# A hybrid attention layer on one Trainium2 core: later slices for one gate weight's preparation, earlier ones for four other weights, and a later first banded score

## The chip, the cores and the metric

The kernel runs on one core of one Trainium2 chip, as one launch. The metric is device time in microseconds (us), the median of several runs; lower is better. One further execution was recorded by the hardware profiler, and all views quoted here are of that execution. Engines carry the profile's names: PE is the matrix engine, PEld its weight load, DVE the vector engine, ACT the scalar engine, POOL the GpSimd engine, SP the engine that only issues transfers. A name with a q behind it (SPq, POOLq) is that engine's issuing side.

## The reference

One decoder layer: an adaLN-modulated RMS norm, one combined input projection, two attention branches with SiLU gates, one output projection, a post-norm and a gated residual. Sizes: 2048 rows, width 1024, head width 64, 8 heads in each branch, 2 key/value heads in the banded one.

```python
mod = jax.nn.silu(c) @ w_ada[l] + b_ada[l]
shift, scale, gate = jnp.split(mod, 3, axis=-1)
h = rms_norm(x, g_pre[l]) * (1.0 + scale[:, None, :]) + shift[:, None, :]
proj = h @ w_in[l]
qa, ka, va, fa, za, qb, kb, vb, zb = jnp.split(proj, split_points, axis=-1)
oa = forgetting_attention(qa, ka, va, fa + b_fgate[l]) * jax.nn.silu(za)   # causal, gate bias
ob = sliding_window_sink_attention(rope(qb), rope(kb), vb, sinks[l]) * jax.nn.silu(zb)  # band of 128
y = jnp.concatenate([oa, ob], axis=-1) @ w_out[l]
x = x + gate[:, None, :] * rms_norm(y, g_post[l])
```

(The head reshapes are left out.)

## The kernel before

**Number format.** Every matmul operand is split into two half-precision parts, high and low, and three products (high by high, high by low, low by high) are added in one accumulation. A weight block of 1024 by 128 (a "key" such as `zb1`, the second tile of the banded branch's gate weight) must therefore be measured and split before its first matmul. Eight steps do this. `w_load` fetches the raw block (POOL's queue, L205). `w_max` takes the largest magnitude of each partition on DVE (L211) and POOL writes these 128 numbers to DRAM (`mx_d`, L214). `w_back` has POOL read them back, spread over all partitions (`mxr`, L219). `w_scale` reduces them to one number on DVE (L230) and makes a power-of-two scale from it (L86 to L237). `w_high` makes the high part on ACT (L245). `w_low`, in two halves, makes the low part on DVE (L251). `w_done` derives a factor from the scale.

**First stage.** The start section computes the modulation, a bound `bmx` on its result (L615, reduced over partitions through two small PE operations), and from it the scale and shift columns `Gp`, `Shp` that ACT applies to the transposed activations (L396). DVE splits the result into `hT` (L400, L401). Then the projections follow in a list `punits` of *slices*. A slice is a handful of matmuls: one eighth of a projection of 512 rows, or one transposition of a later group of 512 rows (`turn_x`). The list begins with 512-row group 0: eight slices of `kb` (slices 0 to 7), eight of `vb` (8 to 15), eight of `zb0` and eight of `zb1`, with eight transposition slices for group 1 set between them, so that `zb1` begins at slice 29 and group 1's `kb` at slice 40.

**What sets the order.** Inside `manual_schedule` the instructions of each engine are issued in the order in which the program writes them, up to small shifts between neighbouring steps. `add` puts the eight steps of a key into `events` at fixed numbers of slices ahead of the key's first slice (the leads). `fill(n, each)` runs n slices, the events of each slice first. `after(k, f)` defers a step by k ticks, and `tick2` ticks at every second slice. Every engine works through its own list strictly in order, so an instruction that waits holds up all that stand behind it on its engine.

**First banded scores.** After the first stage, 32 `windows` (pairs of 128-query blocks) are worked through: `scores` on PE (L831, into `pss`), `maxima` on DVE (L844), `exps` on ACT (L855), `turn` (PE transposes, L864, into `pxb`), `pv` (L883). Between them stand the remaining projection slices. Window 0's scores need the rotated queries `stb`, which come from ACT (high part, L713) and DVE (low part, L706) after a transfer that swaps half-heads (`qs<-qf`, L699) and a POOL product (L711).

Of the kernel before, what the change touches and what calls it, by code (L numbers as in the profile page):

```python
# [40 lines left out]
def hybrid_layer(  # L41
# [158 lines left out]
    def w_load(key, pieces, eng=None):  # L200
        width = VB if key == "vb" else P
        raw = (vbw if key == "vb" else wpool).tile([P, KT, width], F32, tag="wraw", name=f"wr_{key}")
        o = 0
        for col0, n in pieces:
            (eng or G).dma_start(raw[:, :, o:o + n], w_in0[:, col0:col0 + n].rearrange("(k p) n -> p k n", p=P))  # L205
            o += n
        wq[key] = [raw]

    def w_max(key):
        mx = sm(1, "w_mx")  # L210
        V.tensor_reduce(mx[:], wq[key][0][:], axis=AX.XY, op=ALU.max, apply_absolute_value=True)  # L211
        md = mx_d[len(kaps_seen) % 3]
        kaps_seen.append(key)
        G.dma_start(md[:], mx[:])  # L214
        wq[key].append(md)

    def w_back(key):
        mxr = mxp.tile([P, P], F32, tag="mxr", name="mxr")
        G.dma_start(mxr[:], wq[key].pop().rearrange("p o -> (p o)").partition_broadcast(P))  # L219
        wq[key].append(mxr)  # L220

    def w_scale(key):

        floor = key[:2] == "qk"
        raw, mxr = wq[key]
        if key in first:
            mx2 = mxr
        else:
            mx2 = sm(1, "w_mx2")
            V.tensor_reduce(mx2[:], mxr[:], axis=AX.X, op=ALU.max)  # L230
        pw = sm(1, "w_pw")
        pow2_floor(pw[:], mx2[:], "w_p2")
        if floor:
            V.tensor_tensor(pw[:], pw[:], pfl[:], op=ALU.max)
        sw = sm(1, "w_sw")
        V.reciprocal(sw[:], pw[:])
        V.tensor_scalar(sw[:], sw[:], 2.0 ** 14, None, op0=ALU.mult)  # L237
        wq[key] = [raw, pw, sw]

    def w_high(key):  # L240
        raw, pw, sw = wq[key]
        width = VB if key == "vb" else P
        pool = vbw if key == "vb" else wpq if key[0] in "qk" else wpool
        whl = pool.tile([P, 2, KT, width], F16, tag="whl", name=f"wh_{key}")
        A.activation(whl[:, 0], raw[:], AF.Identity, scale=sw[:])  # L245
        wq[key].append(whl)

    def w_low(key, part, parts=2):
        raw, pw, sw, whl = wq[key]
        ks = slice(KT * part // parts, KT * (part + 1) // parts)  # L250
        V.scalar_tensor_tensor(whl[:, 1, ks], raw[:, ks], sw[:], whl[:, 0, ks], op0=ALU.mult, op1=ALU.subtract)  # L251
        if part == parts - 1:
            wq[key] = whl
            pws[key] = pw
# [34 lines left out]
    def pieces(key):  # L289
        kind, j = key[:2], int(key[2:] or 0)  # L290
        if kind == "vb":
            return [(OFF_VB, P), (OFF_FA, 8)]
        if kind == "qk":
            return [(OFF_QA + j * 64, 64), (OFF_KA + j * 64, 64)]
        return [({"qb": OFF_QB, "kb": OFF_KB, "va": OFF_VA, "za": OFF_ZA, "zb": OFF_ZB}[kind] + j * P, P)]
# [604 lines left out]
    def add(key, us):  # L900
        if key not in pkeys and key not in ("kb", "vb"):
            at = len(punits) - (24 if key[:2] == "za" else 0)
            for n, (lead, f) in enumerate(((42, lambda: w_load(key, pieces(key))), (31, lambda: w_max(key)),
                                           (21, lambda: w_back(key)), (12, lambda: w_scale(key)),
                                           (8, lambda: w_high(key)), (6, lambda: w_low(key, 0)),
                                           (4, lambda: w_low(key, 1)), (3, lambda: w_done(key)))):
                if key == "zb0":
                    if n >= 3:
                        events.setdefault(n + 9, []).append(f)
                else:  # L910
                    events.setdefault(max(at - lead, n), []).append(f)
        if key not in pkeys:
            pkeys.append(key)
        punits.extend(us)

    events = {}
    others = []
    for kind, j in (("zb", 0), ("zb", 1), ("va", 0), ("zb", 2), ("zb", 3), ("va", 1), ("va", 2)):
        key = f"{kind}{j}"
# [48 lines left out]
    N_PRO = len(punits)  # L968
# [72 lines left out]

    swa_order = tc.manual_schedule()
    with swa_order:
        fill(N_PRO - 4, tick2)
        psx.close()
        sws = swa_pool("sws", 1)
        ptp = swa_pool("ptp", 1)
        ps_s = swa_pool("ps_s", 1, space=PSUM)
        ps_t = swa_pool("ps_t", 1, space=PSUM)
        ps_pv = swa_pool("ps_pv", 1, space=PSUM)  # L1050
        wsp = swa_pool("wsp", 2)
        wss, wst = sm(16, "a_m"), sm(2, "wst")
        wsq = {}
        base = N_PRO
        NW = len(windows)
        windows[0].scores()
        windows[0].maxima()
        fill(2, tick2)
        windows[0].exps()
        fill(2, tick2)  # L1060
        for n, wd in enumerate(windows):
            goal = base + (N_SWA - base) * (n + 1) // NW
            todo = goal - pos[0]
            part = [todo * (m + 1) // 4 - todo * m // 4 for m in range(4)]
            tick()
            if n:
                wd.maxima()
            fill(part[0])
            tick()
            if n:  # L1070
                wd.exps()
            fill(part[1])
            tick()
            fill(part[2])
            tick()
            fill(part[3])
            if n:
                windows[n - 1].pv()
            wd.turn()
            if n + 1 < NW:  # L1080
                windows[n + 1].scores()

            if n:
                A.activation(wsq[n - 1][:], wsq[n - 1][:], AF.Square, accum_out=wss[:, (n - 1) % 16:(n - 1) % 16 + 1])
            if n == 16:
                V.tensor_reduce(wst[:, 0:1], wss[:], axis=AX.X, op=ALU.add)
            wsq[n] = wsp.tile([P, 2 * P], F32, tag="wsq", name="wsq")
            SP.dma_start(wsq[n][:], w_out0[n // 4 * P:(n // 4 + 1) * P, n % 4 * 2 * P:(n % 4 + 1) * 2 * P])
        tick()
        fill(5)  # L1090
        tick()
        fill(5)
        tick()
        fill(6)
        windows[NW - 1].pv()
        tick()
        tick()
        A.activation(wsq[NW - 1][:], wsq[NW - 1][:], AF.Square, accum_out=wss[:, 15:16])
        V.tensor_reduce(wst[:, 1:2], wss[:], axis=AX.X, op=ALU.add)
        wsum = sm(1, "w_mx2")  # L1100
        V.tensor_reduce(wsum[:], wst[:], axis=AX.X, op=ALU.add)
        pw_ = bk[bank()][:, 0:1]
        PE.matmul(pw_, ones[:], wsum[:], start=True, stop=True)
        root_scale(wrt[:], pw_)
# [493 lines left out]
```

## Time and profile before

| | us |
|---|---|
| median of 3 runs (1217.82 to 1222.75) | 1220.69 |
| the profiled execution's own time | 1218.8 |
| its span, first to last instruction | 1216.6 |
| PE busy | 1158.6 (95%) |
| DVE busy | 904.4 (74%) |
| ACT busy | 674.7 (55%) |
| POOL busy | 142.7 (12%) |

All times of views are counted from the span's start. A row of the timeline gives start, duration, engine, line of the kernel, operation, output and inputs, and in brackets how long the engine stood idle before it and what ended that. PEclk is the share of full clock that PE was granted.

### The profile page before, as it was taken

The numbers are of one execution on the slowest core, as the hardware profiler recorded it, in microseconds if no ns is written. First come the engines' busy times: TensorE is split into PE (matmuls) and PEld (weight loads), VectorE is DVE, ScalarE is ACT, GpSimd is POOL, SyncE is SP. The second block draws the span as 40 slices with busy tenths as digits, with TensorE's granted clock in tenths as the row PEclk, the third lists the DMA queues.
The fourth block names the chain that finished last, engine by engine and source line by source line (L and its number), as shares of the span: only waits on it lengthen the run. The fifth ranks groups of instructions, "written<-read, shape, count | busy, mean of one in ns | idle before, by whom it ended". The sixth has DMA issues, their size and how long they took to land.

```text
span 1216.6 us, 27400 instructions
## 1 busy us (share of the span) xinstructions
PE 1158.6 (95%) x10832; PEld 693.8 (57%) x10832; DVE 904.4 (74%) x2268; ACT 674.7 (55%) x1117; POOL 142.7 (12%) x252
## 2 busy tenths in 40 slices
PE   6599989999999999999999999999999979999997
PEld 2367657655568876555555555555555545555553
DVE  6676657677777647688888798878978797666665
ACT  2675435555555542566666666666766778333231
POOL 2001122233322211010010110010000000000000
PEclk8899999999999999999999999999999989999999
DMA  9645333334322322323334322122111135445652
GB/s 324 204 131 168 82 77 60 67 94 92 96 78 69 57 60 54 72 61 82 83 60 84 86 60 79 39 71 49 39 44 43 58 117 187 144 156 191 198 169 83
DMA packets 88036, 120.71 MB, mean 99 GB/s; under 512 B 27836, under 2 KB 63716, under 8 KB 87908
## 3 DMA queue, kind: packets, MB, share of 16 engines
q1 hardware_dynamic: 76932, 85.94, 24.3%
q0 software_dynamic: 10976, 33.03, 12.0%
q8 instruction: 85, 1.39, 0.6%
q14 instruction: 43, 0.35, 0.1%
HBM read 71.56 MB, written 25.18 MB: 80 GB/s over the span
## 4 chain that ended last, share of the span: by engine, by line
PE 82%; DVE 9%; DMA 5%; issue 2%; ACT 2%; SPq 1%; POOL 0%; DVEq 0%; ACTq 0%; POOLq 0%
PE bk L307 32%; PE bk L1406 13%; PE bk L325 6%; PE sta L1257 4%; PE bk L1208 4%; PE sta L1258 4%; PE poa L1283 2%; PE poa L1284 2%; PE poa L1281 2%; PE pxb L864 2%; PE bk L740 2%; DMA qs<-qf 2%; PE pss L831 2%; PE pob L883 2%; DVE pha L1271 1%
## 5 line engine op out<-in xcount | busy, mean ns | idle before, releaser
L1264 ACT ACTIVATE p<-sta,lift,scl_qk 128x1024 f32<-128x1024 f32 (+2 forms) x160 | 172.0, 1075 | 135.1 <-PE sta L1258 78.7
L307 PE MATMUL bk<-hT,wh_qk 128*128 128x512 f16 x768 | 194.7, 378 | 0.4 <-DVE a_m L1211 0.4
L1406 PE MATMUL bk<-wohl,oz 128*128 128x512 f16 x768 | 172.4, 379 | 1.9 <-ACT wohl L1346 0.8
L1271 DVE TENSOR_TENSOR pha<-p,pha 128x1024 f16<-128x1024 f32 (+2 forms) x160 | 169.1, 1057 | 0.0
L1211 DVE TENSOR_REDUCE a_m<-bk 128x1 f32<-128x512 f32 x192 | 130.2, 686 | 52.3 <-PE bk L1208 51.7
L1268 ACT ACTIVATE pha<-p 128x1024 f16<-128x1024 f32 (+2 forms) x160 | 148.0, 925 | 6.4 <-PE poa L1284 1.3
L1406 PEld LDWEIGHTS <-oz 128*128 128x128 f16 x768 | 74.4, 99 | 83.9 <-issue 1.8
L1281 PE MATMUL poa<-vt,pha 128*128 128x65 f16 x1088 | 117.4, 193 | 2.7 <-DVE ona L1290 2.7
L1284 PE MATMUL poa<-vt,pha 128*128 128x65 f16 x1088 | 117.1, 193 | 1.1 <-DVE pha L1271 1.1
L1283 PE MATMUL poa<-vt,pha 128*128 128x64 f16 x1088 | 117.4, 195 | 0.0
L1257 PE MATMUL sta<-T 128*128 128x512 f16 (+1 forms) x320 | 112.2, 351 | 4.7 <-ACT p L1264 4.6
L307 PEld LDWEIGHTS <-wh_qk 128*128 128x128 f16 x768 | 72.4, 97 | 75.3 <-issue 1.4
L1208 PE MATMUL bk<-T 66*128 66x512 f16 (+2 forms) x320 | 109.8, 349 | 2.9 <-DMA T<-stq 2.4
L1281 PEld LDWEIGHTS <-pha 128*128 128x128 f16 x1088 | 102.4, 97 | 17.4 <-DVE ona L1290 3.8
L1258 PE MATMUL sta<-T 69*128 69x512 f16 (+1 forms) x320 | 111.1, 352 | 0.0
L1283 PEld LDWEIGHTS <-pha 128*128 128x128 f16 x1088 | 101.5, 97 | 11.5 <-issue 0.3
L1284 PEld LDWEIGHTS <-pha 128*128 128x128 f16 x1088 | 101.5, 99 | 1.3 <-DVE pha L1271 1.3
L307 PE MATMUL bk<-hT,wh_za 128*128 128x512 f16 x384 | 99.8, 378 | 0.0
L325 PE MATMUL bk<-wh_va,hT 128*128 128x128 f16 x1536 | 93.0, 221 | 2.6 <-DVE wh_va L251 2.3
L325 PEld LDWEIGHTS <-hT 128*128 128x128 f16 x1536 | 89.1, 99 | 8.3 <-issue 5.4
L307 PE MATMUL bk<-hT,wh_zb 128*128 128x512 f16 x384 | 89.8, 379 | 0.0
L307 PE MATMUL bk<-hT,wh_qb 128*128 128x512 f16 x384 | 87.4, 379 | 0.0
(491 smaller groups left out, 1872.4 us busy)
## 6 DMA issues: line engine op xcount, KB each, us to landing
wa<-in_w_ada_dram SPq DMA_DIRECT2D x16, 512.0 KB
z_d<-tz POOLq DMA_DIRECT2D x32, 256.0 KB, 2.7
T<-stq SPq DMA_DIRECT2D x128, 64.0 KB
T<-o_d SPq DMA_DIRECT2D x16, 512.0 KB
T<-z_d SPq DMA_DIRECT2D x16, 512.0 KB
xr<-in_x_dram SPq DMA_DIRECT2D x16, 512.0 KB
out_dram<-yg SPq DMA_DIRECT2D x15, 512.0 KB
xt<-in_x_dram SPq DMA_DIRECT2D x12, 512.0 KB
```

What stands on the lines that cost most here:

```text
L307: PE.matmul(ps, whl[:, a, k, :], hT[ci][:, b, k, :], start=(k == 0 and n == 0), stop=(k == KT - 1 and n == 2))
L325: PE.matmul(ps[:, u * P:(u + 1) * P], hT[ci][:, a, k, u * P:(u + 1) * P], whl[:, b, k, :], start=(k == 0 and n == 0), stop=(k == KT - 1 an ...
L1208: PE.matmul(mx[:, :w], T[0:XM, 0, i * P:(i + 1) * P], T[0:XM, 2, pc * CH:pc * CH + w], start=True, stop=True)
L1257: PE.matmul(self.st[:, o:o + w], T[:, 3, kb_], T[:, 1, qc], start=True, stop=False)
L1258: PE.matmul(self.st[:, o:o + w], T[0:XR, 2, kb_], T[0:XR, 0, qc], start=False, stop=not diag)
L1264: A.activation(self.p32[:, :self.w], self.st[:, :self.w], AF.Exp, scale=scl[f"qk{self.hd}"][:], bias=lift[:])
L1268: A.activation(self.ph[:, 0, :self.w], self.p32[:, :self.w], AF.Copy)
L1271: V.tensor_tensor(self.ph[:, 1, :self.w], self.p32[:, :self.w], self.ph[:, 0, :self.w], op=ALU.subtract)
L1281: PE.matmul(po[:, u, :], ph[:, 0, pq], vt[:, b, hd, 0:65], start=(self.first and n == 0 and u == 0), stop=False)
L1283: PE.matmul(po[:, u, 0:64], ph[:, 0, pq], vt[:, b, hd, 65:VW], start=False, stop=False)
L1284: PE.matmul(po[:, u, :], ph[:, 1, pq], vt[:, b, hd, 0:65], start=False, stop=(self.last and n == len(self.blocks) - 1))
L1406: PE.matmul(py, self.hl[:, i, k, :], w_slot(8 * j + k)[:, cc], start=(k == 0 and m_ == 0), stop=(k == KT - 1 and m_ == 2))
```

## The change

Three edits. `zb1` gets slices of its own: its load moves from slice 0 to 2, `w_max` from 1 to 12, `w_back` from 3 to 14, `w_scale` from 12 to 20, `w_high` from 16 to 23, the two `w_low` from 18 and 20 to 25 and 26, `w_done` from 21 to 27; its first matmul stays at slice 29. For the value weights `va0` to `va3` and the gate weights `zb2` and `zb3`, `w_scale` to `w_done` run at leads 14, 10, 8, 7, 5 where they ran at 12, 8, 6, 4, 3. And window 0's scores and maxima stand two slices later (two slices before the end of the first stage, not four), while the two slices behind its exponentials fall away there; the number of slices is the same.

```diff
-            for n, (lead, f) in enumerate(((42, lambda: w_load(key, pieces(key))), (31, lambda: w_max(key)),
-                                           (21, lambda: w_back(key)), (12, lambda: w_scale(key)),
-                                           (8, lambda: w_high(key)), (6, lambda: w_low(key, 0)),
-                                           (4, lambda: w_low(key, 1)), (3, lambda: w_done(key)))):
+            leads = (42, 31, 21, 14, 10, 8, 7, 5) if key[:2] in ("va", "zb") else (42, 31, 21, 12, 8, 6, 4, 3)
+            fs = (lambda: w_load(key, pieces(key)), lambda: w_max(key), lambda: w_back(key), lambda: w_scale(key),
+                  lambda: w_high(key), lambda: w_low(key, 0), lambda: w_low(key, 1), lambda: w_done(key))
+            for n, f in enumerate(fs):
                 if key == "zb0":
                     if n >= 3:
                         events.setdefault(n + 9, []).append(f)
+                elif key == "zb1":
+                    events.setdefault((2, 12, 14, 20, 23, 25, 26, 27)[n], []).append(f)
                 else:
-                    events.setdefault(max(at - lead, n), []).append(f)
+                    events.setdefault(max(at - leads[n], n), []).append(f)
...
     with swa_order:
-        fill(N_PRO - 4, tick2)
+        fill(N_PRO - 2, tick2)
...
         windows[0].maxima()
         fill(2, tick2)
         windows[0].exps()
-        fill(2, tick2)
```

Where the instructions stand, in three places on DVE. The first is the start section, where the bound `bmx` is made; `wr_zb_561` is `zb1`'s raw block:

```order
 L611 SCALAR_TENSOR_TENSOR abss<-shf 128x8
 L613 SCALAR_TENSOR_TENSOR bnd<-absg,abss 128x8
-L211 TENSOR_REDUCE w_mx<-wr_zb_561 128x1
 L615 TENSOR_REDUCE bmx<-bnd 128x1
 L619 TENSOR_REDUCE bm<-bk_134 1x1
```

The maximum of `zb1` no longer stands between the two steps that make the bound. The second place is where the scale of `zb0` has just been made (L237). Before, the reduction of `zb1`'s read-back `mxr` (L230) came next:

```order
L237 TENSOR_SCALAR w_sw<-w_sw 128x1
L230 TENSOR_REDUCE w_mx_663<-mxr 128x1
L86 TENSOR_SCALAR w_p_666<-w_mx_663 128x1
L87 TENSOR_SCALAR w_pw<-w_p_666 128x1
L236 RECIPROCAL w_sw<-w_pw 128x1
L237 TENSOR_SCALAR w_sw<-w_sw 128x1
L752 SCALAR_TENSOR_TENSOR vb<-bk_135,vb 128x2x64 x2
```

Now, from the same L237 on (`wr_zb_567` is `zb1`'s raw block, `qs` the product that POOL makes at L711):

```order
L237 TENSOR_SCALAR w_sw<-w_sw 128x1
L211 TENSOR_REDUCE w_mx<-wr_zb_567 128x1
L752 SCALAR_TENSOR_TENSOR vb<-bk_135,vb 128x2x64 x2
L754 SCALAR_TENSOR_TENSOR fl<-bk_135,kf,bfg 128x16
L251 SCALAR_TENSOR_TENSOR wh_zb_689<-wr_zb_287,w_sw,wh_zb_689 128x512 x2
L285 TENSOR_SCALAR cz_zb_731<-w_pw,pH 128x1
L287 TENSOR_TENSOR fac_129<-kap_vb,cz_zb_731 128x1
L712 TENSOR_TENSOR qc<-qc,qs 128x512
L401 TENSOR_TENSOR hT_105<-hf,hT_105 128x512
L752 SCALAR_TENSOR_TENSOR vb<-bk_136,vb 128x2x64 x2
L754 SCALAR_TENSOR_TENSOR fl<-bk_136,kf,bfg 128x16
L230 TENSOR_REDUCE w_mx_767<-mxr 128x1
```

The maximum stands here, and the reduction of what comes back ten rows behind it. The halves of `zb1`'s low part (L251), which stood just behind this place, now follow eight rows behind that reduction. POOL's order does not move: the load of `zb1`, the write of its maxima (L214), their read-back (L219), then the product L711. The third place is window 0's maxima (L844, closed by L848). Before, from the last of them on:

```order
L844 ISA b_m 128x1
L848 TENSOR_SCALAR b_nb<-b_m 128x4
L230 TENSOR_REDUCE w_mx_1922<-mxr 128x1
L86 TENSOR_SCALAR w_p_1925<-w_mx_1922 128x1
L87 TENSOR_SCALAR w_pw<-w_p_1925 128x1
L236 RECIPROCAL w_sw<-w_pw 128x1
L237 TENSOR_SCALAR w_sw<-w_sw 128x1
L712 TENSOR_TENSOR qc<-qc,qs 128x512
```

Now, from the query product L702 on, which stood ahead of the first of them:

```order
L702 SCALAR_TENSOR_TENSOR qc<-bk_134,cosT 128x512
L230 TENSOR_REDUCE w_mx_1872<-mxr 128x1
L86 TENSOR_SCALAR w_p_1875<-w_mx_1872 128x1
L87 TENSOR_SCALAR w_pw<-w_p_1875 128x1
L236 RECIPROCAL w_sw<-w_pw 128x1
L237 TENSOR_SCALAR w_sw<-w_sw 128x1
L844 ISA sm__1927,b_m<-pss,bmask,snk,scl_qb_1658 128x128
```

The reduction of `va0`'s read-back and the scale made from it have moved from behind the window's maxima to ahead of them. On ACT, `va0`'s high part (L245) likewise moves ahead of window 0's exponentials.

## The prediction

> **What bounds the kernel now.** I read the page first, then PE's waits over the whole span, then the timeline of each engine around the waits that the change touches.
>
> ```profile
> span 1216.6 us, 27400 instructions
> PE 1158.6 (95%) x10832; PEld 693.8 (57%) x10832; DVE 904.4 (74%) x2268; ACT 674.7 (55%) x1117; POOL 142.7 (12%) x252
> PE bk L617 <- DVE bmx L615: 7.8, 1, 7.8
> PE bk L325 <- DVE wh_va L251: 2.3, 1, 2.3
> PE pss L831 <- ACT stb L713: 1.3, 1, 1.3
> PE pss L831 <- DVE stb L706: 0.4, 1, 0.4
> 80.00:160.00 80.00, 80.00 (x619) 1.00 0.46 119
> ```
>
> PE is the bound: 95% busy, and without a gap from 80 to 160 us (the last row gives length, busy time and granted clock of that stretch). A delay of PE in the first stage is therefore carried to the end, and a wait removed there is earned to the end. Four waits of PE (us in total, times, longest) lie where the change reaches: 7.8 for the bound `bmx`, 2.3 for `va0`'s low part, 1.3 and 0.4 for window 0's queries. The working below is against the profiled execution's own 1218.8 us (span 1216.6), which lies 1.9 under the median of 1220.69.
>
> **Part 1: the bound no longer waits for `zb1`.** DVE first, then ACT:
>
> ```profile
> 44.99 0.17 DVE L613 SCALAR_TENSOR_TENSOR bnd<-absg,abss 128x8 f32<-128x8 f32 x1
> 50.15 1.22 DVE L211 TENSOR_REDUCE w_mx<-wr_zb 128x1 f32<-128x1024 f32 x1 [4.99 <-DMA wr_zb<-in_w_in_dram]
> 51.29 0.15 DVE L615 TENSOR_REDUCE bmx<-bnd 128x1 f32<-128x8 f32 x1
> 47.98 1.19 ACT L245 ACTIVATE wh_vb<-wr_vb,w_sw 128x1088 f16<-128x1088 f32 x1
> 53.90 0.78 ACT L396 ACTIVATE hT<-px,Shp,Gp 128x512 f16<-128x512 f32 x1 [4.74 <-DVE pfl L627]
> ```
>
> `w_max` of `zb1` waits 4.99 us for its block, and the bound's last reduction queues behind it. With `w_max` gone, `bmx` starts at about 45.1, 6.2 earlier. Only part of that arrives: ACT, which makes the activations from the bound, is busy with `vb`'s high part until 47.98 + 1.19 = 49.17. That is next in line, so L396 moves from 53.90 to about 49.2: **-4.7 us**. From there to `vb` the pace is set by ACT and DVE, so all rows up to `zb0` move by the same 4.7. The load of `zb1` itself moves nowhere, since it is still next in POOL's order and waits for the same buffer.
>
> **Part 2: `zb1`'s scale is now made in a hurry.** The chain from the maximum to the scale leaves the core twice. POOL's and DVE's rows, and the two transfers' landing times over all 23 keys (mx_d, then mxr):
>
> ```profile
> 51.67 0.56 POOL L214 DMA_DIRECT2D mx_d<-w_mx  x1 [9.02 <-DVE bmx L615]
> 60.33 0.54 POOL L219 DMA_DIRECT2D mxr<-mx_d  x1 [8.11 <-DMA mx_d<-w_mx]
> 125.96 1.21 DVE L211 TENSOR_REDUCE w_mx<-wr_qb 128x1 f32<-128x1024 f32 x1
> 135.20 0.54 POOL L219 DMA_DIRECT2D mxr<-mx_d  x1 [4.92 <-DMA mx_d<-w_mx]
> 140.24 0.29 DVE L230 TENSOR_REDUCE w_mx<-mxr 128x1 f32<-128x128 f32 x1 [5.10 <-DMA mxr<-mx_d]
> 165.23 0.54 POOL L219 DMA_DIRECT2D mxr<-mx_d  x1
> 170.51 0.29 DVE L230 TENSOR_REDUCE w_mx<-mxr 128x1 f32<-128x128 f32 x1 [2.83 <-DMA mxr<-mx_d]
> DMA to landing us min/median/max: 8.1/8.3/9.8
> DMA to landing us min/median/max: 4.4/5.0/6.7
> ```
>
> Where DVE waited for it throughout, the way from the start of `w_max` to that of L230 took 140.24 - 125.96 = 14.3 us. Put together from `zb1`'s own first half (60.33 - 50.15 = 10.2) and `va0`'s second half (170.51 - 165.23 = 5.3) it is 15.5. I take 14.9, between the two. The ends: 135.20 - 125.96 = 9.2 and the shortest read-back, 4.4, make 13.6; from `w_max` to the issue 51.67 - 50.15 = 1.5, and the longest landings, 9.8 and 6.7, make 18.0. The change gives this chain slices 12 to 20. The Trainium skill prices it otherwise: "DMA: Bandwidth & Descriptors", section "Anatomy of one DMA — SWDGE (gpsimd) path", fits a transfer from POOL as 2.0 us plus its bytes at 436 GB/s, which makes an estimate of 1.5 + 2.0 + 2.2 = 5.7 us for the chain and would leave almost no wait in this part. The rows above speak against it by a factor of two to four; its case is the first rival.
>
> Now the place where it is wanted:
>
> ```profile
> 68.59 0.28 DVE L230 TENSOR_REDUCE w_mx<-mxr 128x1 f32<-128x128 f32 x1
> 69.47 0.15 DVE L237 TENSOR_SCALAR w_sw<-w_sw 128x1 f32<-128x1 f32 x1
> 69.16 1.28 POOL L711 TENSOR_TENSOR qs<-qs,sinT 128x512 f32<-128x512 f32 x1 [8.29 <-DMA qs<-qf]
> 72.02 0.69 DVE L712 TENSOR_TENSOR qc<-qc,qs 128x512 f32<-128x512 f32 x1
> 75.41 0.68 DVE L706 TENSOR_TENSOR stb<-qc,stb 128x512 f16<-128x512 f32 x1
> 76.46 1.29 DVE L401 TENSOR_TENSOR hT<-hf,hT 128x512 f16<-128x512 f32 x2
> 73.23 0.74 DVE L251 SCALAR_TENSOR_TENSOR wh_zb<-wr_zb,w_sw,wh_zb 128x512 f16<-128x512 f32 x1
> 76.95 1.46 PE L307 MATMUL bk<-hT,wh_zb 128*128 128x512 f16 x6
> ```
>
> `w_max` takes L230's old place, 68.59 - 4.7 = 63.9, so L230 can start at 63.9 + 14.9 = 78.8. Behind it, before the first half of `zb1`'s low part is done, stand five small steps (69.47 + 0.15 - 68.59 = 1.0), `stb`'s L706, one L400 and two L401 (which ran in this order before too, 76.46 + 1.29 - 75.41 = 2.3) and L251 itself (0.74): 4.1 us, so 82.9. ACT's high part (1.14) is hidden in that. PE's third matmul of `zb1` is the first that needs the low part. It is the sixth of the group at 76.95, whose starts lie 0.22 apart: 78.0 before, and 78.0 - 4.7 = 73.3 if nothing held it. PE therefore waits until 82.9: **+9.6 us**, which takes back part 1 and 4.9 more. DVE would not be free much earlier anyway: POOL's L711 stands behind the read-back's issue (0.54, at about 63.9 + 9.7 = 73.6) and takes 1.28, so L712 and all behind it on DVE wait to about 75.4, where before it ran at 72.02. Behind DVE, ACT's `stb` and the next group's transposed activations are late by about 5 too. They are wanted at group 1's `kb`, which is late by as much, so they add nothing.
>
> **Part 3: the clock after a long wait.** Stretches give length, PE busy, clock, DMA share:
>
> ```profile
> 175.20:177.60 2.40, 0.07 (x3) 0.95 0.17 67
> 177.60:180.60 3.00, 3.00 (x29) 0.50 0.52 141
> 177.59 6.92 PE L325 MATMUL bk<-wh_va,hT 128*128 128x128 f16 x94 [2.33 <-DVE wh_va L251]
> 194.96 4.86 PE L325 MATMUL bk<-wh_va,hT 128*128 128x128 f16 x84
> ```
>
> After 2.3 us of standing still PE was granted half its clock for about 3 us, and 94 matmuls took 6.92 where the later row's pace gives 94 x 4.86 / 84 = 5.4: a loss of 1.5. A wait of 9.6 will cost that too: **+1.5** (0 if the group behind were held by ACT anyway, 3.0 if two such stretches follow).
>
> **Part 4: window 0.** PE, ACT and DVE in turn:
>
> ```profile
> 164.47 0.28 PE L831 MATMUL pss<-kst,stb 64*128 64x128 f16 x4 [1.34 <-ACT stb L713]
> 165.19 0.56 PE L831 MATMUL pss<-kst,stb 64*128 64x128 f16 x8 [0.44 <-DVE stb L706]
> 173.46 0.82 PE L864 MATMUL pxb<-ident,sm__1912 128*128 128x128 f32 x6
> 169.05 0.49 ACT L855 ACTIVATE sm__1912<-sm__1912,b_nb 128x257 f32<-128x257 f32 x1
> 165.79 0.41 DVE L844 CUSTOM_DVE_ANT_0 sm__1912<-pss,bmask,snk 128x128 f32<-128x128 f32 x1
> ```
>
> All in times of before, since everything here moves with PE. Two slices (1.3 us) ahead of the scores cover the 1.34, and most of the 0.44 stays. But DVE now waits for `va0`'s read-back ahead of the maxima. That lands at 170.5 as before, for POOL's order is the same. The scale ends 1.0 later, the maxima start at 171.6 in place of 165.79, 5.8 later, and the last exponential, which ended at 169.5, ends at 175.3. PE reaches the transposes (L864) at 173.46 - 1.3 = 172.1 and waits to 175.3 for the last of them. Then some 0.6 until the transposes end and about 0.8 for window 1's scores put `va0` at 176.7. Its low part, behind the maxima and two rows of 0.7 on DVE, is there by then. Before, it went on at 177.59: **-0.9**. Whether a wait of about 2 to 3 us, partly filled, halves the clock again is an even chance, so half of the 1.5 of before is earned: **-0.7**. The Trainium skill ("TensorE: Matmul & The Clock Gate", "Part 1: The HAM clock gate") asks for an idle window of about 3.4 us before the clock falls; by it this term would be -1.5. The 2.3 us above that sufficed speaks for the milder value. Bounds of this part: -2.4 and 0.
>
> **Part 5: the other weights.** `va1` to `va3`, `zb2`, `zb3` meet the same reduction earlier on DVE. PE waits for none of their parts before. What a window step costs that DVE brings late is bounded by the one that did:
>
> ```profile
> PE pob L883 <- DVE ptb L869: 1.4, 1, 1.4
> ```
>
> I take a third of it, since some eight slices of projections stand between a window's maxima and its transposes: **+0.5** (0 to 1.4).
>
> The sum is -4.7 + 9.6 + 1.5 - 0.9 - 0.7 + 0.5 = +5.3: 1224.1 against 1218.8. On the median that is 1226.0. With every term at its better end it is -4.7 + 8.3 + 0 - 2.4 + 0 = +1.2 (1221.9), at its worse end -4.7 + 12.7 + 3.0 + 0 + 1.4 = +12.4 (1233.1).
>
> **The rivals.** *The read-back is in time.* The chain then ends before DVE gets to L230 and PE keeps the 4.7: -4.7 - 1.6 + 0.5 = -5.8, 1214.9. This ends on the other side. It decides where the chain is at most 14.9 - 9.6 = 5.3 us; against it stand all 23 landings, whose shortest pair is 8.1 + 4.4. The page of the Trainium skill cited above, "DMA: Bandwidth & Descriptors", would have it so. Chance 0.08.
>
> *The read-back is later still.* In times of after, `zb1`'s two transfers meet the loads of the next rows of x, which kept the transfer engines 97% busy before:
>
> ```profile
> 77.60:84.00 6.40, 6.40 (x37) 1.00 0.97 277
> ```
>
> With landings of 9.8 and 6.7 the wait grows by 3.1, a second half-clock stretch adds 1.5, and window 0 gives nothing (1.6 less): +5.3 + 6.2 = +11.5, 1232.2. It decides where L230 starts after about 81. For it: the transfers in that stretch. Against it: 170.51 came 5.3 after its issue beside other traffic. Chance 0.25.
>
> *Window 0 pays in full.* If the swapped queries land sooner in the new timing, all four of its costs go (1.34 + 0.44 + 2.33 + 1.5 = 5.6) in place of 1.6: +5.3 - 4.0 = +1.3, 1222.0. Against it: nothing in POOL's order moves there. Chance 0.09.
>
> **How the numbers follow.** The forecast has 0.58: 1226.0, its own range 1222 to 1230. A measurement of this kernel can tell about 0.5% (6.1 us) from no change, so "slower" begins at 1226.8 and "faster" ends at 1214.6. Of the forecast 0.23 lies above 1226.8, with the second rival's 0.24 makes slower 0.47. Of the first rival 0.05 is beyond the other bound. The rest, 0.48, is the same within 0.5%. The range 1218 to 1233 leaves out the first rival and the far end of the second.
>
> **What would show it.** In the profile after: `bmx` right behind `bnd` at about 45.1 and the first L396 at 49.2 (part 1); L219 waiting for `mx_d` to about 74 and L230 with a wait on `mxr` to about 79 (part 2); a PE wait of some 8 to 10 us, split between ACT's high part and DVE's low part of `zb1`, followed by about 3 us at half clock (part 3); no wait of PE for `va0`, and a new one at L864 of 2 to 3 us (part 4). I am wrong if PE runs through `zb1` without a wait, or if its unbroken stretch to 160 absorbs the delay.

## The result, and the profile after

The changed kernel took 1225.81 us in the median (1221.92 to 1231.80, 20 runs), the kernel before 1220.22 beside it on the same chip (1216.74 to 1223.38, 20 runs): 1.0049 times as long, 95% interval 1.0036 to 1.0061. The forecast was 1226.0; 5.6 us is just inside the 6.1 that the prediction counts as no change to be told. The profiled execution took 1225.7 us with a span of 1223.5, against 1218.8 and 1216.6: 6.9 us more. From about L905 on, a line of the changed kernel has a number one higher than the same line before.

The page's head:

```profile
span 1223.5 us, 27396 instructions
PE 1161.8 (95%) x10832; PEld 694.4 (57%) x10832; DVE 906.5 (74%) x2268; ACT 674.6 (55%) x1117; POOL 141.4 (12%) x252
```

PE's waits over the span (us in all, times, longest):

```profile
PE bk L307 <- ACT wh_zb L245: 9.1, 1, 9.1
PE pob L883 <- DVE ptb L869: 3.0, 2, 2.1
PE bk L617 <- DVE bmx L615: 1.7, 1, 1.7
PE bk L307 <- DVE wh_zb L251: 0.7, 1, 0.7
```

The wait for `bmx` has gone from 7.8 to 1.7 us. A wait of 9.1 for `zb1`'s high part and 0.7 for its low part stand in its place. The waits for `va0` (2.3) and for window 0's queries (1.3 and 0.4) are gone, and one of 2.1 for window 2's `ptb` is new.

The bound, on DVE and then ACT; these answer to 51.29 and 53.90 before:

```profile
45.19 0.16 DVE L615 TENSOR_REDUCE bmx<-bnd 128x1 f32<-128x8 f32 x1
49.12 0.76 ACT L396 ACTIVATE hT<-px,Shp,Gp 128x512 f16<-128x512 f32 x1
```

`zb1`'s scale, in the timelines of DVE, POOL and ACT, in order of time:

```profile
63.78 1.21 DVE L211 TENSOR_REDUCE w_mx<-wr_zb 128x1 f32<-128x1024 f32 x1
65.29 0.56 POOL L214 DMA_DIRECT2D mx_d<-w_mx  x1 [22.64 <-DVE w_mx L211]
73.69 0.54 POOL L219 DMA_DIRECT2D mxr<-mx_d  x1 [7.85 <-DMA cosT<-cs__241]
74.25 1.27 POOL L711 TENSOR_TENSOR qs<-qs,sinT 128x512 f32<-128x512 f32 x1
75.56 0.69 DVE L712 TENSOR_TENSOR qc<-qc,qs 128x512 f32<-128x512 f32 x1 [8.39 <-POOL qs L711]
79.80 0.29 DVE L230 TENSOR_REDUCE w_mx<-mxr 128x1 f32<-128x128 f32 x1 [2.41 <-DMA mxr<-mx_d]
83.03 1.41 DVE L251 SCALAR_TENSOR_TENSOR wh_zb<-wr_zb,w_sw,wh_zb 128x512 f16<-128x512 f32 x2
```

The maximum is made at 63.78 and comes back at 79.80, 16.0 us later. On the way POOL waits until 73.69 before it may issue the read-back, and its multiply L711 stands behind that; DVE stands still for 8.39 us for that product, and 2.41 more for the read-back itself. So two chains end late at almost the same place. By the fit in the Trainium skill ("DMA: Bandwidth & Descriptors", section "Anatomy of one DMA — SWDGE (gpsimd) path") this way is estimated at 5.7 us; the 16.0 us contradict it.

PE there, in the timeline after, down to the first `kb` matmul of group 1:

```profile
82.08 1.03 PE L307 MATMUL bk<-hT,wh_zb 128*128 128x512 f16 x2 [9.12 <-ACT wh_zb L245]
83.83 0.61 PE L307 MATMUL bk<-hT,wh_zb 128*128 128x512 f16 x1 [0.71 <-DVE wh_zb L251]
92.39 2.97 PE L307 MATMUL bk<-hT,wh_kb 128*128 128x512 f16 x13
```

The same matmul in the timeline before:

```profile
84.09 5.34 PE L307 MATMUL bk<-hT,wh_kb 128*128 128x512 f16 x24
```

Stretches of PE after (length, PE busy, clock, DMA share and GB/s):

```profile
82.00:88.40 6.40, 5.60 (x17) 0.50 0.35 83
92.40:168.00 75.60, 75.60 (x594) 1.00 0.41 110
```

Group 1 starts 8.3 us later than before, and PE then runs without a gap to 168, so these 8.3 reach window 0 whole. There and at window 2, PE and POOL in the timeline after, and the last row, a stretch of PE (its clock is the 0.53):

```profile
172.64 0.67 PE L831 MATMUL pss<-kst,stb 64*128 64x128 f16 x12
180.46 0.93 PE L864 MATMUL pxb<-ident,sm__1927 128*128 128x128 f32 x4 [0.17 <-ACT sm__1927 L855]
182.08 5.53 PE L325 MATMUL bk<-wh_va,hT 128*128 128x128 f16 x96
187.45 0.81 PE L307 MATMUL bk<-hT,wh_qb 128*128 128x512 f16 x3
197.97 1.24 PE L883 MATMUL pob<-vb,ptb 128*128 128x64 f16 x22 [2.07 <-DVE ptb L869]
201.97 1.24 PE L325 MATMUL bk<-wh_va,hT 128*128 128x128 f16 x19
167.73 1.25 POOL L711 TENSOR_TENSOR qs<-qs,sinT 128x512 f32<-128x512 f32 x1 [9.08 <-DMA qs<-qf]
193.56 0.54 POOL L219 DMA_DIRECT2D mxr<-mx_d  x1 [8.49 <-DMA qs<-qf]
197.90:201.50 3.60, 3.53 (x36) 0.53 0.00 0
```

Two of these rows in the timeline before:

```profile
184.35 0.81 PE L307 MATMUL bk<-hT,wh_qb 128*128 128x512 f16 x3
161.77 1.26 POOL L711 TENSOR_TENSOR qs<-qs,sinT 128x512 f32<-128x512 f32 x1 [10.66 <-DMA qs<-qf]
```

The scores, the transposes and `va0` run with a single wait of 0.17. The `qb` matmuls behind `va0` start at 187.45, before at 184.35. Of the 8.3 us lost 3.1 are left, so window 0 earned 5.2. Ten microseconds on, most of it is given back: POOL waits 8.49 us for swapped queries ahead of a read-back, the chain behind it is late, PE waits 2.07 and runs at half clock to 201.5. `va0`'s next matmuls start at 201.97 where they started at 194.96 before (that row is in the prediction): 7.0 behind again, and 6.9 at the end of the span.

### The profile page after: what moved, and what is told of

It reads as the page before. It is cut to its first block, busy times and chain, and to the rows that moved or that the text cites. A ratio compares the mean times of both kernels' runs of the same rounds, so it can differ in the third digit from the quotient of the medians.

```text
span 1223.5 us, 27396 instructions
## 1 busy us (share of the span) xinstructions
PE 1161.8 (95%) x10832; PEld 694.4 (57%) x10832; DVE 906.5 (74%) x2268; ACT 674.6 (55%) x1117; POOL 141.4 (12%) x252
## 4 chain that ended last, share of the span: by engine, by line
PE 79%; DVE 9%; DMA 4%; issue 3%; SPq 2%; ACT 2%; POOL 1%; DVEq 0%; POOLq 0%; ACTq 0%
PE bk L307 31%; PE bk L1407 13%; PE bk L325 6%; PE sta L1258 4%; PE bk L1209 4%; PE sta L1259 4%; PE poa L1284 2%; PE poa L1285 2%; PE poa L1282 2%; PE pxb L864 2%; PE pss L831 2%; PE pob L883 2%; DVE pha L1272 2%; DVE a_m L1212 1%; PE bk L1370 1%
## 5 line engine op out<-in xcount | busy, mean ns | idle before, releaser
L307 PE MATMUL bk<-hT,wh_qk 128*128 128x512 f16 x768 | 194.7, 379 | 0.4 <-DVE a_m L1212 0.4
L307 PEld LDWEIGHTS <-wh_qk 128*128 128x128 f16 x768 | 72.4, 97 | 75.2 <-issue 1.4
L307 PE MATMUL bk<-hT,wh_zb 128*128 128x512 f16 x384 | 92.4, 386 | 9.8 <-ACT wh_zb L245 9.1
L307 PE MATMUL bk<-hT,wh_za 128*128 128x512 f16 x384 | 99.9, 379 | 0.0
L307 PE MATMUL bk<-hT,wh_qb 128*128 128x512 f16 x384 | 87.4, 380 | 0.0
```

Source lines behind the costliest of these rows:

```text
L307: PE.matmul(ps, whl[:, a, k, :], hT[ci][:, b, k, :], start=(k == 0 and n == 0), stop=(k == KT - 1 and n == 2))
```

## The experiments

All further runs were on chips on which the kernel before takes 1214.5 to 1214.8 us, about 5.5 less than on the first. So only ratios are compared with the first pair, and traces by the way from the first L396 to `kb` of group 1 ("kb1"), which is 30.2 us before and 43.3 after. Theory 1 is the prediction's own: the changed slices are too few for `zb1`'s way through memory. Theory 2 puts the loss on the other two edits, theory 3 on ACT and DVE having too much to do at `zb1`, whatever brings the scale.

| kernel | first L396 | kb1 starts | between | median us | times before (95%) |
|---|---|---|---|---|---|
| before, first chip | 53.90 | 84.09 | 30.2 | 1220.22 | 1 |
| whole change, first chip | 49.12 | 92.39 | 43.3 | 1225.81 | 1.0049 (1.0036 to 1.0061) |
| before, again | 53.72 | 84.63 | 30.9 | 1214.5 | 1 |
| whole change, again | 48.95 | 92.61 | 43.7 | 1220.37 | 1.0055 (1.0037 to 1.0072) |
| `zb1`'s events alone | 48.64 | 91.09 | 42.5 | 1221.42 | 1.0053 (1.0037 to 1.0068) |
| other two edits alone | 54.05 | 84.24 | 30.2 | 1213.38 | 0.9992 (0.9980 to 1.0004) |
| extra matmuls in the wait | 49.10 | 89.11 | 40.0 | 1217.41 | 1.0017 (1.0006 to 1.0028) |
| maximum on the chip | 48.62 | 79.33 | 30.7 | 1227.18 | 1.0102 (1.0082 to 1.0121) |
| the same, transfers kept | 48.67 | 88.91 | 40.2 | 1217.40 | 1.0028 (1.0015 to 1.0041) |
| maximum six slices sooner | 48.56 | 81.08 | 32.5 | 1212.26 | 0.9988 (0.9969 to 1.0006) |
| maximum in the start | 48.72 | 81.23 | 32.5 | 1210.96 | 0.9979 (0.9966 to 0.9993) |
| the same, smoothed | 48.79 | 79.84 | 31.1 | 1211.26 | 0.9972 (0.9957 to 0.9986) |
| leads alone | 53.53 | 84.14 | 30.6 | 1216.43 | 1.0017 (1.0006 to 1.0029) |
| window alone | 53.54 | 83.72 | 30.2 | 1214.35 | 0.9999 (0.9987 to 1.0011) |

### Which edit costs

The first edit alone, against the changed kernel:

```diff
-            leads = (42, 31, 21, 14, 10, 8, 7, 5) if key[:2] in ("va", "zb") else (42, 31, 21, 12, 8, 6, 4, 3)
+            leads = (42, 31, 21, 12, 8, 6, 4, 3)
...
-        fill(N_PRO - 2, tick2)
+        fill(N_PRO - 4, tick2)
...
         windows[0].exps()
+        fill(2, tick2)
```

> Only zb1's events are moved (slices 2, 12, 14, 20, 23, 25 to 27); the leads of the other weights and the start of window 0 are as before. Theory 1 (zb1's way through memory, about 16 us from its maximum to its scale, now ends after PE wants its low part): the bound goes on at 45.2 and the first L396 at 49.2, PE then waits some 9 us for zb1's high part with about half the clock behind it, kb1 starts 8.3 us later than before, and nothing is earned at window 0: 1220.2 + 8.3 = about 1228.5, so slower than the whole change. Theory 2 (the loss of the whole change comes from the other two edits, where the scale of va0 stands ahead of window 0's maxima, and zb1 is hidden): no PE wait at zb1 and 1215 to 1220.

The other two edits alone:

```diff
-                    events.setdefault((2, 12, 14, 20, 23, 25, 26, 27)[n], []).append(f)
+                    events.setdefault((0, 1, 3, 12, 16, 18, 20, 21)[n], []).append(f)
```

> The other two edits without the first: the leads of va and zb weights two slices sooner and window 0's scores two slices later; zb1's events as before. Theory 1: the first 160 us are as before (bmx at 51.3, kb1 at about 84.1); from window 0 on it earns about 5.2 us and gives about 3.9 of it back at window 2, as in the whole change: about 1219, at best 1215 if the giving back hangs on the shift of 8.3 us. Theory 2: the two edits are what costs, and it comes out at 1225 or more.

PE's longest wait with the first edit alone:

```profile
PE bk L307 <- ACT wh_zb L245: 8.8, 1, 8.8
```

PE at window 0 with the other two, in the timeline:

```profile
172.72 0.93 PE L864 MATMUL pxb<-ident,sm__1927 128*128 128x128 f32 x4 [0.17 <-ACT sm__1927 L855]
174.34 5.53 PE L325 MATMUL bk<-wh_va,hT 128*128 128x128 f16 x96
```

The first edit brings the wait with it and costs 0.53%, 6.4 us on 1214.8. That is less than the 8.3 expected, but all that its kb1 is late: 91.09 against 84.63 in the kernel before's second trace, 6.5 us. The wait is as long as in the whole change; the matmuls behind it are done sooner here (7.4 us from the third matmul of `zb1`, at 83.73, to kb1, in place of 92.39 - 83.83 = 8.6), because the half clock ended earlier, before 86.8. The other two bring no wait above 0.2 here and cost nothing: 0.9992, with 1 in the interval. Theory 2 falls.

### Both kernels again on a second chip

> The kernel before, unchanged, for its trace beside those of the variants on the same chip. The variants so far ran where the kernel before takes 1214.8 and not 1220.2. Every theory expects the same waits as in its first trace: PE 6 to 8 us for bmx, then none until window 0's queries. If window 0's waits (1.3 + 0.4 + 2.3 with half a clock behind, 5.6 in all) are a matter of when the swapped queries land, they may be smaller here; if they are fixed by the order of the program, they are the same 5.6.

> The whole change, unchanged, for its trace beside the others'. Expected: 5 to 6 us over the kernel before; PE's wait of about 9 us at zb1 and the half clock behind it as in the first trace, since the chain through memory is 16 us long on any chip. The wait of 2.1 at window 2 (ptb, behind swapped queries that land late) is there again if it follows from the order, and may be gone if it is a chance meeting of transfers.

Two of PE's waits in the kernel before, on this chip:

```profile
PE bk L617 <- DVE bmx L615: 7.0, 1, 7.0
PE bk L325 <- DVE wh_va L251: 2.3, 2, 1.9
```

One in the whole change:

```profile
PE bk L307 <- ACT wh_zb L245: 8.8, 1, 8.8
```

POOL's product ahead of window 0 in the kernel before, on this chip:

```profile
160.03 1.26 POOL L711 TENSOR_TENSOR qs<-qs,sinT 128x512 f32<-128x512 f32 x1 [8.68 <-DMA qs<-qf]
```

The costs that come from the program's order are there again: 7.0 for `bmx` (7.8 in the first trace), 2.3 for `va0`, 8.8 at `zb1` (9.1). Window 0's waits for its queries (1.3 and 0.4) are absent in the kernel before here, so they hung on when the swapped queries landed. In the first trace of the kernel before they landed late: L711 starts 161.77 - 84.09 = 77.7 us behind kb1 there, 160.03 - 84.63 = 75.4 here in the same kernel, 167.73 - 92.39 = 75.3 in the first trace of the change, and between 73.7 and 76.2 in all other traces. In the whole change PE does not wait at window 2 here; its longest wait for `ptb`, 1.4, stands at 230 us, where the kernel before had one of the same length in its first trace. So what was given back at window 2 was a meeting of transfers in one trace, and does not follow from the order. The kernel before was traced here in an execution of 1218.04 us, 3.5 above its median, so the spans of these two traces are not compared, only their rows up to window 2.

### The half clock

The whole change, with matmuls whose result is overwritten in PE's idle time:

```diff
+    def keep_warm():
+        ps = bk[next(n for n in order_ if n not in held)][:]
+        for _ in range(40):
+            PE.matmul(ps, wq["zb0"][:, 0, 0, :], hT[0][:, 0, 0, :], start=True, stop=True)
+
+    at_slice(29, keep_warm)
```

> The whole change, with 40 extra 128x512 matmuls of data that is at hand into a bank that is overwritten next, placed where PE stands still for zb1 (about 8.7 us of work in a wait of 9.1). Theory 1 (of the 8.3 us lost at kb1 about 2.5 are matmuls at half clock behind the wait): the clock stays at 1.00 in 83 to 89 us, zb1's remaining matmuls take about 2.5 us less, and the time is about 1223.3. Rival: ACT and DVE set the pace behind the wait anyway, so the clock costs nothing: 1225 to 1226, or up to 1227 where the extra matmuls last longer than the wait.

PE in the wait and behind it (length, PE busy, clock, DMA share and GB/s):

```profile
74.00:83.00 9.00, 8.01 (x38) 1.00 0.66 237
83.00:88.40 5.40, 5.36 (x31) 1.00 0.40 115
```

The third matmul of `zb1` in the timeline:

```profile
83.04 0.39 PE L307 MATMUL bk<-hT,wh_zb 128*128 128x512 f16 x1 [1.03 <-DVE wh_zb L251]
```

PE is kept from waiting, the clock stays at 1.00, and from the third matmul of `zb1` to kb1 it takes 89.11 - 83.04 = 6.1 us in place of 92.39 - 83.83 = 8.6. The half clock costs 2.5 us in the first trace, as expected. Against the same 6.1 it costs 2.8 in the second trace of the whole change (92.61 - 83.70 = 8.9) and 1.3 with the first edit alone (7.4), so its size moves from trace to trace though the wait does not. The whole gain is larger, 1.0017 against 1.0049 and 1.0055, 3.9 to 4.6 us. Some 0.8 of that is a read-back that lands sooner in this trace; the rest wasn't followed up.

### The scale without the way through memory

The maximum reduced over the partitions by a transpose and a matmul with ones (declarations, and the same exception in the read-back and scale steps, left out):

```diff
     def w_max(key):
+        if key == "zb1":
+            V.tensor_reduce(mx1[:], wq[key][0][:], axis=AX.XY, op=ALU.max, apply_absolute_value=True)
+            return
...
+    def z1_row():
+        z1["ps"] = ps_x.tile([P, CH], F32, tag="x", name="px")
+        PE.transpose(z1["ps"][0:1, 0:P], mx1[:], ident[:])
+        V.tensor_reduce(mz1[:], z1["ps"][0:1, 0:P], axis=AX.X, op=ALU.max)
+
+    def z1_all():
+        PE.matmul(z1["ps"][:, P:P + 1], ones[0:1, :], mz1[:], start=True, stop=True)
+        V.tensor_copy(mx1[:], z1["ps"][:, P:P + 1])
+        wq["zb1"].append(mx1[:])
+
+    at_slice(16, z1_row)
+    at_slice(19, z1_all)
```

> The whole change, but zb1's maximum is taken over the partitions on the chip (a transpose and a reduction at slice 16, a matmul with ones and a copy at slice 19) in place of the two transfers through memory; everything else keeps its slice. Theory 1: the bound's gain (4.7) stays and PE's wait at zb1 and its half clock go, 8.3 + 4.7 = 13.0 us sooner at kb1 than the whole change less at most 1 us for the two small PE steps: about 1213 to 1216. Theory 3 (what holds PE at zb1 is that ACT and DVE have too much to do between vb and zb1, whatever brings the scale): the wait stays at 7 us or more, and about 1224 to 1226.

The same, but the write of the maxima and their read-back stay in POOL's queue, for nothing:

```diff
         if key == "zb1":
             V.tensor_reduce(mx1[:], wq[key][0][:], axis=AX.XY, op=ALU.max, apply_absolute_value=True)
+            md = mx_d[len(kaps_seen) % 3]
+            kaps_seen.append(key)
+            G.dma_start(md[:], mx1[:])
+            wq[key].append(md)
             return
...
         G.dma_start(mxr[:], wq[key].pop().rearrange("p o -> (p o)").partition_broadcast(P))
+        if key == "zb1":
+            return
```

> As the on-chip maximum of zb1, but the write of the maxima and the broadcast read of them are kept as transfers whose result nobody uses, so that POOL's queue, the three buffers of each and all later keys' turns are as in the whole change. The on-chip variant started kb1 12.6 us sooner than the whole change and lost it again by stalls of all engines in the second stage (5.0 at 447, 5.0 at 575, 8.0 at 847 us). Theory A (those stalls come from the shifted turn of the buffers and of POOL's transfers): they go, and the time is about 7 us under the kernel before. Theory B (they come from the few more PE and DVE instructions or from the shifted time): they stay, and it is 10 to 13 us over it.

Without the transfers, kb1 (its L314 is L307) in the timeline:

```profile
79.33 5.34 PE L314 MATMUL bk<-hT,wh_kb 128*128 128x512 f16 x24
```

Without them, two of PE's waits over the span, both in the second stage:

```profile
PE poa L1307 <- issue: 5.9, 3, 3.1
PE bk L1231 <- DMA T<-rw: 5.0, 1, 5.0
```

With the transfers kept, POOL, DVE and PE in the timeline (L228, L722, L723, L318 are L219, L711, L712, L307):

```profile
72.98 0.54 POOL L228 DMA_DIRECT2D mxr<-mx_d  x1 [7.40 <-DMA cosT<-cs__243]
73.54 1.27 POOL L722 TENSOR_TENSOR qs<-qs,sinT 128x512 f32<-128x512 f32 x1
74.84 0.69 DVE L723 TENSOR_TENSOR qc<-qc,qs 128x512 f32<-128x512 f32 x1 [7.76 <-POOL qs L722]
79.29 1.68 PE L318 MATMUL bk<-hT,wh_zb 128*128 128x512 f16 x3 [6.08 <-ACT wh_zb L256]
```

Without them PE runs through `zb1`, and kb1 starts at 79.33, 13.06 us sooner than in the first trace of the whole change; 13.0 was expected. ACT and DVE do the same scaling and splitting at the same slices, so theory 3 falls. The kernel is slower all the same, by stalls far behind (last section). Kept transfers take those stalls away (theory A), but 1.0028 is not the 7 us under the kernel before that was expected: PE waits again, 6.08 us, though the scale no longer needs the read-back. POOL may issue that only at 72.98, its multiply stands behind it, and DVE, which makes the scale, stands behind the multiply. So of the 9.8 us that PE waits in the whole change, about 6 are there by POOL's order alone, since the read-back's issue waits for the write to land; the late scale adds the rest.

### Sooner by a known amount

The write and the read-back six slices sooner, all else as changed:

```diff
-                    events.setdefault((2, 12, 14, 20, 23, 25, 26, 27)[n], []).append(f)
+                    events.setdefault((2, 6, 8, 20, 23, 25, 26, 27)[n], []).append(f)
```

> The whole change, but zb1's maximum and read-back six slices sooner (6 and 8 in place of 12 and 14), about 5.2 us sooner on DVE; scale and splits stay at slices 20 to 27. Theory 1 (PE's wait is the length of the way through memory less the slices it has, both over L230 and over POOL's rotation multiply behind the read-back's issue): the wait of 9 us becomes about 4, kb1 starts 37 to 38 us behind the first L396 (43.3 in the whole change, 30.2 before), and the time is 0 to 1 us over the kernel before: 1.000. Rival (the cost is that DVE and ACT are given zb1's scale and splits at slices 20 to 27 at all): the wait stays near 9 and the time 1.005.

DVE, POOL, DVE and PE in this variant:

```profile
58.31 1.20 DVE L211 TENSOR_REDUCE w_mx<-wr_zb 128x1 f32<-128x1024 f32 x1
66.81 0.54 POOL L219 DMA_DIRECT2D mxr<-mx_d  x1 [6.44 <-DMA mx_d<-w_mx]
70.97 0.28 DVE L230 TENSOR_REDUCE w_mx<-mxr 128x1 f32<-128x128 f32 x1 [0.37 <-DMA mxr<-mx_d]
75.01 0.39 PE L307 MATMUL bk<-hT,wh_zb 128*128 128x512 f16 x1 [1.14 <-DVE wh_zb L251]
```

It moved further than expected, 32.5 and not 37 to 38. The maximum is 5.5 us sooner (58.31 against 63.78), the way is 12.7 us long in place of 16.0, and with a wait of only 1.14 the half clock is gone too: 5.5 + 3.3 + 2.5 = 11.3, and kb1 is 92.39 - 81.08 = 11.3 sooner. So a start 5.5 us sooner earned twice that in this trace: the transfers also landed faster, and the shorter wait left the clock up. How the landings depend on the start is not shown. The time, 0.9988, can't be told from the kernel before.

Then the maximum in the start section, behind the bound, with `zb1`'s other events as before; and the same with two steps moved apart:

```diff
         for k in range(KT):
...
+            if k == 0:
+                w_load("zb1", pieces("zb1"))
+            if k == 1:
+                w_max("zb1")
...
-                    events.setdefault((2, 12, 14, 20, 23, 25, 26, 27)[n], []).append(f)
+                    if n >= 2:
+                        events.setdefault((0, 1, 3, 12, 16, 18, 20, 21)[n], []).append(f)
```

> The other two edits as changed, and zb1 with the events of before, but its load and its maximum moved into the start block: the maximum stands behind the second pair of transposes' splits, where the bound no longer queues behind it and where its block has landed (about 50 to 51 us). Theory 1 (only the length of the way through memory matters: 16 us from the maximum to L230, which needs to be over by about 69): the bound goes on at 45, the first L396 at 49.2, PE has no wait at zb1, kb1 starts 4.7 us sooner than before and 13 sooner than in the whole change: 0.995 of the kernel before, about 6 us less. Rival: zb1's load in the start makes its POOL or DVE steps block the first activations (the maximum waits for the block in front of them), and 2 to 5 us of the gain go: 0.997 to 1.000.

```diff
-            if k == 2:
+            if k == 4:
                 V.tensor_reduce(mxs[:, 2:3], wq["zb0"][0][:], axis=AX.XY, op=ALU.max, apply_absolute_value=True)
...
-                        events.setdefault((0, 1, 3, 12, 16, 18, 20, 21)[n], []).append(f)
+                        events.setdefault((0, 1, 3, 17, 18, 20, 21, 22)[n], []).append(f)
```

> As the variant with zb1's maximum in the start block, with its two small stumbles taken out: zb0's own reduction (1.2 us, two splits behind zb1's) moves two splits later, and zb1's scale stands behind zb0's low part in place of ahead of it. Theory 1: the first kb group's splits and zb0's low part are no longer late, so kb1 starts 30.2 to 30.7 us behind the first L396 in place of 32.5, and the time is about 2 us less than the variant's: 0.996 of the kernel before. Rival: the second reduction only moves the stumble to a later split of the same group: 0.998 as before.

The first of them loses part of its gain, about as much as its rival said but by another way. Its first L396 is not late (48.72). PE waits for the low part of `zb0`, which stands behind `zb1`'s scale on DVE (at 66.72), and that scale waited for its read-back:

```profile
65.17 0.28 DVE L230 TENSOR_REDUCE w_mx<-mxr 128x1 f32<-128x128 f32 x1 [0.83 <-DMA mxr<-mx_d]
68.24 0.39 PE L307 MATMUL bk<-hT,wh_zb 128*128 128x512 f16 x1 [1.30 <-DVE wh_zb L251]
```

The second has no such wait and starts kb1 1.4 us sooner. That came from the scale's new place: `zb0` begins 17.6 us behind the first L396 in both (66.34 and 66.42 on PE), so moving the reduction earned nothing by itself, as the rival there said. The times of the two (0.9979 and 0.9972) can't be told apart. Both beat the kernel before (by 2.5 and 3.4 us on 1214.5) and the whole change. A kb1 that comes sooner is not carried on whole, though. In the second, PE at window 0:

```profile
169.09 0.71 PE L868 MATMUL pxb<-ident,sm__1927 128*128 128x128 f32 x2 [0.99 <-ACT sm__1927 L859]
171.91 6.81 PE L325 MATMUL bk<-wh_va,hT 128*128 128x128 f16 x96
```

PE waits for the transposes (L868 is L864), because the maxima stand behind `va0`'s read-back, and its clock is at half behind that (0.56 granted from 172 to 175 us): 6.81 in place of 5.53. Beside the other two edits alone, whose window 0 is the same, kb1 is 84.24 - 79.84 = 4.4 us sooner and the `qb` matmuls behind `va0` only 179.71 - 178.55 = 1.2.

### The leads and the window, apart

Each is the changed kernel with `zb1`'s events as before, and the window's start, or the leads, as before.

> Only the leads of va and zb weights are two slices sooner; zb1's events and window 0's start as before. kb1 30.2 us behind the first L396 as before. va0's low part is there in time, so its wait of 2.3 goes; in its place the scale stands ahead of window 0's maxima on DVE or close to them, and PE waits up to 2 at the transposes. Forecast's reckoning: 0 to 1.5 us less than before (0.999 to 1.000). Rival (the maxima behind the read-back cost more than va0's wait did): 1 to 3 us more.

> Only window 0 is moved: its scores and maxima two slices later; zb1's events and all leads as before. kb1 30.2 us behind the first L396. The two slices hide the queries' landing (1.3 + 0.4 where PE waits for it at all), va0's low part is still late by about 2: forecast's reckoning 0 to 1.5 us less than before (0.999 to 1.000), about the same as the leads alone, and the two together the 1.4 us less that both showed. Rival (the moves only pay together): this one alone 1 to 3 us more, since the two slices that stood between the maxima and the transposes are gone.

PE at window 0 with the leads alone:

```profile
172.54 0.71 PE L864 MATMUL pxb<-ident,sm__1921 128*128 128x128 f32 x2 [0.89 <-ACT sm__1921 L855]
176.91 5.41 PE L325 MATMUL bk<-wh_va,hT 128*128 128x128 f16 x94 [1.58 <-DVE wh_va L251]
```

And with the window alone:

```profile
174.85 0.83 PE L325 MATMUL bk<-wh_va,hT 128*128 128x128 f16 x12 [0.86 <-DVE wh_va L251]
```

With the leads alone both waits are there, since the maxima stand behind the read-back and PE gets to the transposes before them: 1.0017, its rival's side. With the window alone about half of `va0`'s wait is left (0.86, and 0.44 more right behind it): 0.9999. Together neither wait is left (the rows of the other two edits, above). So the two edits pay as a pair if at all; 0.9992 doesn't show a gain.

## Why the prediction was right, point by point

**Part 1** (-4.7): the first L396 moved by 4.78, to 49.12 where 49.2 was forecast. ACT's high part of `vb` was next in line, as said.

**Part 2** (+9.6): L230 came at 79.80 where 78.8 was forecast, since the read-back took 6.1 us from its issue and not 5.3; the third matmul of `zb1` at 83.83 where 82.9 was forecast. PE waited 9.8 in the two parts named. That DVE would not be free much earlier, because of POOL's L711 behind the read-back's issue, was said as an aside; the kept transfers show that it alone makes about 6 of these 9.8.

**Part 3** (+1.5): too small for the first trace. The half clock cost 2.5 there (extra matmuls in the wait), since 0.50 was granted for 6.4 us behind the wait and not for 3. The other traces with this wait gave 2.8 and 1.3, so 1.5 lies within what this cost can be. Parts 1 to 3 thus make +8.3 at kb1 where the sum had 6.4.

**Part 4** (-1.6): both its size and the step it rests on failed. I let L230 of `va0` start at 170.5 of before's time and put a PE wait of 2 to 3 us at L864. The swapped queries landed 2.3 us sooner against PE (167.73 - 8.3 = 159.4 where L711 started at 161.77), POOL's queue behind them moved up, L230 came at 176.09 - 8.3 = 167.8, and PE waited 0.17. This is what the third rival gave for this place: 5.2 of its 5.6 us. But the change did not bring the sooner landing, as that rival supposed: the unchanged kernel has it in its second trace (75.4 us behind kb1, after the change 75.3). The late one was peculiar to the trace that the sum was made against. In the second pair of traces window 0 earned 8.0 - (187.42 - 183.09) = 3.7 us, `va0`'s wait and the half clock behind it; that too is more than 1.6. The wait at L864 does stand in other traces (0.99 smoothed, 0.89 with the leads alone), always under the 2 to 3 us given to it.

**Part 5** (+0.5, bound 1.4): too small for the first trace, which is the one the sum is made against. Window 2 gave back 7.0 - 3.1 = 3.9 us, a wait of 2.07 with half the clock behind it, while its bound had been taken from a wait without that. The Trainium skill ("TensorE: Matmul & The Clock Gate", section "Part 1: The HAM clock gate") asks for an idle window of about 3.4 us. The 0.53 granted behind 2.07 us of waiting speaks against it a second time, and the slow matmuls behind 0.99 and 0.16 us of waiting, in the smoothed variant, a third time.

Parts 4 and 5 together were forecast at -1.1 and came to 3.1 - 8.3 + 3.9 = -1.3 at window 2 of the first pair, two wrong sizes that nearly cancel, and to (198.11 - 193.70) - 8.0 = -3.6 in the second pair. The part ahead of it, 8 us at kb1, came back each time.

That the median came within 0.2 us of the forecast is luck. Profiled execution against profiled execution, which is what the sum is about, the change cost 6.9 us and not 5.3; the 1.6 between them come from parts 1 to 3, which were 1.9 short. The execution profiled before happened to be 1.4 us faster than the median of its 20 runs, so the medians differ by 5.6 only, and their interval (4.4 to 7.4 us) can't tell 5.3 from 6.9. What is shown is the mechanism of parts 1 to 3 and a cost of that order.

**The first rival**, a read-back in time, needed a way of at most 5.3 us (the estimate of 5.7 would have left a wait of 0.4); it took 16.0, and 12.7 at its shortest for `zb1` in these runs. **The second** needed L230 after about 81; it came at 79.80.

## What to carry to other kernels

Count a step that leaves the core backward from its first consumer: here 13 to 16 us from the maximum to the reduction of what comes back, and the queue that issues the return counts with everything behind it, even if nobody needs the result. A wait can often be removed by moving its cause a few steps behind the waiting point in place of to the far end of its slack: the maximum just behind the bound kept the gain, and 0.997 to 0.998 came of it. And add to the price of a PE wait the slow matmuls that can stand behind it. Here they cost 1.3 to 2.8 us, behind waits from about 1 us up, but not behind each of them: the wait of 1.14 above was followed by none.

## What the runs showed of the hardware that I had not expected

The same kernel took 1220.2 us on one chip and 1214.5 to 1214.8 on three others; the change's ratio was the same (1.0049 and 1.0055).

With `zb1`'s two transfers gone, PE stood still in the second stage for 5.0 us (for `T`) and 5.9 in all for nothing that the profile shows. With the two transfers kept, these waits were gone and the span 11.4 us shorter (1213.6 against 1225.0), though kb1 started 9.6 later. The sooner start alone does not bring them: the smoothed variant starts kb1 at 79.84, with the transfers in place, and has none of these waits. So they hang on the transfers, as far as one trace of each can show it; whether by the turn of the three buffers, by the count of POOL's transfers or otherwise is open.

Matmuls on data at hand held the granted clock at 1.00 through a wait of 9 us, and that alone took back about 2.5 us of the loss. How long the half clock lasts behind one and the same wait differs from trace to trace: at 88.0 to 89.2 us PE was granted 0.62 in the first trace of the whole change, 0.50 in the second, and 1.00 with the first edit alone.
